# Two accumulator banks from the other pool, a later close, and a fourth weight buffer in a two-layer encoder trunk

## The chip, the cores and the metric

The kernel runs on one core of a Trainium2 chip. The metric is the device time of one execution in microseconds (us), as the median of several runs; smaller is better. The engines are named as in the profile: PE is TensorE (its matmuls), PEld its weight loads, DVE is VectorE, ACT is ScalarE, POOL is GpSimd, and SP is SyncE, which here issues the DMAs.

## The reference

The reference computes two layers of an encoder on 272 tokens (16 learned ones and 256 of the input), 2048 wide, in float32:

```python
def _layer(h, w_in, ..., w_out, ln1_w, ln1_b, w_ff1, w_ff2, ln2_w, ln2_b):
    proj = jnp.einsum('bld,dp->blp', h, w_in)
    ...
    gq, gk, gv, gr, glr, nq, nk, nv = jnp.split(proj, points, axis=-1)
    y_gla = _gla_mixer(gq, gk, gv, gr, glr, gla_w_up, gla_b_up, gla_norm_w)
    y_na = _na_mixer(nq, nk, nv, na_rel_bias).astype(h.dtype)
    mix = jnp.einsum('blm,md->bld', jnp.concatenate([y_gla, y_na], axis=-1), w_out)
    h = _layer_norm(DEEPNORM_ALPHA * h + mix, ln1_w, ln1_b)
    ff = jnp.einsum('blf,fd->bld', jnp.square(jax.nn.relu(jnp.einsum('bld,df->blf', h, w_ff1))), w_ff2)
    return _layer_norm(DEEPNORM_ALPHA * h + ff, ln2_w, ln2_b)
```

`_gla_mixer` is a gated linear attention in both directions with 4 heads (keys 128 wide, values 256 wide). Its output is divided by the root of its mean square over the 256 values of a head and multiplied by a gate. `_na_mixer` is a neighbourhood attention with 16 heads of 64 on a grid of 4 rows by 64 columns; the 16 learned tokens are further keys, and attend among themselves. The learned tokens are dropped from the output, so that the second layer computes most things for 256 tokens only.

## The kernel before

**Weights.** Each weight matrix comes as tiles of 128 by 1024 float32, 512 KB (eight blocks of 128 by 128). `made` (L187) asks for a tile on SP's queue (`raw`), and `halves` (L215) splits it: ACT rounds it to `wh` (L218), DVE computes the rest `wl = raw - wh` (L219). Activations are split in the same way, and a product is made of three matmuls: high by high, high by low, low by high. `raw`, `wh` and `wl` have three buffers each. `weights` (L181) keeps two tiles made: when the matmuls of a tile are written into the program, the next tile's DMA and its two splitting instructions stand ahead of them, and no later tile's.

**Loops.** `by_m` (L317) makes 128 output columns at a time: eight input blocks per tile, one PSUM bank of the pool `pm`, then an eviction. `by_k` (L279) makes 512 output columns at once in four banks and runs over the input blocks two at a time. It stands where the inputs become ready one after the other: the first group of a layer, the first group of the output projection (`w_out`, in the first layer at L304, in the second through `dense`, L314), and one group of the MLP. PSUM has eight banks: four in the pool `pm` (named mm in the profile) and four in the pool `pb` (named bg), which `bank` (L77) hands out.

**Work in between.** Attention is written as generators in two queues. `gla_head` stands in `bg`, and `na_pair`, `silu` and the norms stand in `fg`. `pump` (L127) is called after each weight tile and runs a few steps of both. A step that yields True says that the next one begins with matmuls that wait for results just asked for; the pump then tries to let a weight tile pass between. A bg step's DVE instructions are kept behind the latest `wl` (`issue_after`, L119).

**The end of the attention.** `layer` runs six groups of `by_m` over the projections of the neighbourhood attention. Ahead of the last of these (g == 5) it runs all steps that are left in `bg`, closes the memory of the linear attention (`gctx.close`, L408), and opens that of the norms (`ln_open`, L409), in which `acc` lies. Then comes `by_k(self.y, n, self.mixed)` (L413): `mixed` (L417) runs one step of `fg` ahead of each pair of input blocks, and writes `acc` (L424). While `alone` is true, `spare` (L80) takes the banks of the attention scores from `pm`, else from `pb`. The pump after the last tile of the sixth group runs the output of pair 5 (`na_out`, L851) and the scores of pair 7 (L778), so that the scores' two banks are the latest of `pm` when `by_k` begins. The score banks are read by DVE at L787 and L789; the bank of the last projection tile is read by ACT at L540 and by DVE at L541.

**One head's norm.** In `gla_head` the two halves of a head are squared by ACT into `grs` and `gtn` (L721), multiplied by the gate on DVE (L723), and the squares are added by DVE (L725). `mean` (L976) splits the sum (`sp`: ACT L339, DVE L340) and multiplies it by a matrix of 1/256 on PE (L983).

**The neighbourhood attention's softmax.** `softmax` (L752) takes the maximum on DVE (L754), the exponentials on ACT (L756), the reciprocal on DVE (L757), and multiplies (L760): on POOL for the grid tokens (tiles `ns` and `npr`), on DVE for the learned tokens (tile `nms`, 16 by 96, first layer only). PE transposes `nms` at L808 together with the values (L805, L806).

Of the kernel before, what the change touches and what calls it, by code (L numbers as in the profile page):

```python
# [14 lines left out]
P = 128  # L15
D = 2048
# [42 lines left out]
class Trunk:  # L59
    def __init__(self, ctx, tc, ins, out):  # L60
        self.ctx, self.tc, self.nc = ctx, tc, tc.nc
        self.i, self.out = ins, out
        self.bg, self.fg, self.credit, self.fcredit = deque(), deque(), 0, 0
        self.wants, self.due, self.late, self.low = {}, deque(), 0, True
        self.x = [None] * DC
        self.stream, self.ready = self.order(), deque()
        pool = lambda name, **k: ctx.enter_context(tc.tile_pool(name=name, **k))
        self.cp = pool("const", bufs=1)
        self.xp = pool("xhl", bufs=1)
        self.yp = pool("yhl", bufs=1)  # L70
        self.wp = pool("wst", bufs=3)
        self.jp = pool("jn", bufs=1)
        self.pm = pool("pm", bufs=4, space=PSUM)
        self.pb = pool("pb", bufs=4, space=PSUM)
        self.hp = pool("hop", bufs=2, space=bass.MemoryType.DRAM)
# [8 lines left out]
    def consts(self):  # L84
        nc, c = self.nc, self.cp
        t = lambda n, s, d=F32: c.tile(s, d, name=n, tag=n)
        t("pad", [P, PAD])
        self.vec = t("vec", [P, DEPTH, 66])
        nc.sync.dma_start(self.vec, self.i["vec"].rearrange("l p v -> p l v"))
        self.ident = t("ident", [P, P])  # L90
        nc.sync.dma_start(self.ident, self.i["ident"])
        self.sel = t("sel", [LRK, 2])
        nc.sync.dma_start(self.sel, self.i["sel"])
        self.qmask = t("qmask", [NM, NK2])
        nc.sync.dma_start(self.qmask, self.i["qmask"])
        self.mask = t("mask", [P, 5, 32], U8)
        raw = self.xr.tile([P, 2, L], F32, name="xraw", tag="xraw", bufs=3)[:, 0, :5 * 32].rearrange("p (l c) -> p l c", l=5)
        nc.sync.dma_start(raw, self.i["mask"])
        nc.gpsimd.tensor_copy(self.mask, raw)
        self.ones = {}  # L100
        for n in (GDV, 4 * P, D):
            self.ones[n] = t(f"ones{n}", [P, P])
            nc.gpsimd.memset(self.ones[n], 1.0 / n)
        self.ones_r = {}
        for n in self.ones:
            self.ones_r[n] = t(f"onesr{n}", [P, P], F32R)
            nc.scalar.copy(self.ones_r[n], self.ones[n])
        self.eps = t("eps", [P, 1])
        nc.gpsimd.memset(self.eps, EPS)
        self.one = t("one", [P, 1])  # L110
        nc.gpsimd.memset(self.one, 1.0)
# [68 lines left out]

    def weights(self):  # L181

        while len(self.ready) < 2:
            self.ready.append(self.made(*next(self.stream, (None, (), None))))
        return self.ready.popleft()

    def made(self, ap, ends, kind):  # L187
        if ap is None:
            return None
        nc = self.nc  # L190
        raw = self.wp.tile([P, WB], F32, name="raw", tag="raw")
        wh, wl = (self.wp.tile([P, WIDE], F32R, name=nm, tag=nm) for nm in ("wh", "wl"))
        wh, wl = self.blocks(wh, *HIGHS[kind]), self.blocks(wl, *LOWS[kind])
        for c in map(slice, (0,) + ends, ends):
            self.asked = nc.sync.dma_start(raw[:, c], ap[:, c]).ins
            self.halves(raw[:, c], wh, wl, slice(c.start // P, c.stop // P))
        if not ends:
            self.head(ap, raw, wh, wl)
        return wh, wl
# [76 lines left out]
        self.nc.vector.tensor_tensor(t, t, parts[0], ALU.add)  # L276
        return t

    def by_k(self, acts, n, before, wide=False):  # L279

        ps = [self.pm.tile([P, 512], F32, name="mm", tag="mm") for _ in range(4)]
        if wide:
            ps += [self.bank() for _ in range(4)]
        nk = len(acts)
        for k in range(0, nk, 2):
            before(k)
            if n == T:
                self.dense(ps, acts[k:k + 2], self.weights(), k)
                continue
            for g in range(0, len(ps), 4):  # L290
                wh, wl = self.weights()
                parts = ((wh, 0), (wh, 1), (wl, 0))
                order = [(j, p, m) for j in range(2) for p in range(3) for m in range(4)]
                first = wide and not k
                if first and not g:
                    order.sort(key=lambda o: (o[0], o[2] // 2))
                elif wide and k == 2 and not g:
                    order.sort(key=lambda o: o[1])
                elif first:
                    order.sort(key=lambda o: o[1] // 2)  # L300
                else:
                    order.sort(key=lambda o: (k and o[2], o[1] // 2, o[2]))
                for j, p, m in order:
                    self.nc.tensor.matmul(ps[g + m][:, :n], lhsT=self.block(parts[p][0], 4 * j + m if first else 2 * m + j), rhs=acts[k + j][parts[p][1]][:, :n],  # L304
                                          start=k + j + p == 0, stop=k == nk - 2 and j + p == 3)
        return [[p[:, :T], p[:, T:]] if n == T else [p[:, :n]] for p in ps]
# [46 lines left out]
    def layer(self, l):  # L353
# [4 lines left out]
        with ExitStack() as actx:  # L358
# [20 lines left out]
            with ExitStack() as ectx:  # L379
                self.ep = pool("early", "right", ectx)  # L380
                self.fcredit = 0
                self.fg.append(self.gates())
                if l == 0:
                    with ExitStack() as xctx:
                        self.xr = pool("xr", "right", xctx)
                        first = self.by_k(self.x, L, self.load_x, wide=True)
                    for m in range(4):
                        self.ev_k(m, first.pop(0)[0])
                for m, ps in enumerate(first):
                    self.ev_v(m, ps[0])  # L390
                self.credit, self.alone = 0, True
                self.by_m(self.x, [L] * 4, lambda m, ps: self.ev_v(4 + m, ps), pump=(1, 1, True))
                self.by_m(self.x, [n] * 4, self.ev_q, pump=(1, 1, True))
                self.drain()
            self.a2 = pool("na", "left", bufs=2)
            with ExitStack() as gctx:
# [5 lines left out]
                    self.by_m(self.x, [n] * 4, lambda m, ps: self.ev_r(4 * g + m, ps), pump=(1, GLA_R))  # L402
                self.na_tiles()
                for g in range(6):
                    if g == 5:
                        while self.bg:
                            self.step(self.bg, 1)
                        gctx.close()  # L408
                        self.ln_open()  # L409
                    ns = [n if (4 * g + m) % 3 == 0 else L for m in range(4)]  # L410
                    self.by_m(self.x, ns, lambda m, ps: self.ev_na(4 * g + m, ps), pump=(1, GLA_NA, True))
            self.alone = False
            ps = self.by_k(self.y, n, self.mixed)  # L413
            self.drain()
        self.tail(ps)

# [163 lines left out]
    def gla_head(self, h):  # L580
# [141 lines left out]
            os_.append(g2.tile([P, L], F32, name="on", tag="on")[:, :n])  # L722
            nc.vector.tensor_tensor(os_[e], o, self.gate[2 * h + e], ALU.mult)  # L723
        yield
        nc.vector.tensor_tensor(rs, rs, tn, ALU.add)  # L725
        ms = yield from self.mean(rs, GDV, pool=g2)
        self.newton(rs, ms, self.eps, tn)
        yield
# [8 lines left out]
    def na_tiles(self):  # L737

        def t(name, *shape):
# [4 lines left out]
        self.fetch = lambda: None  # L744
        self.nv = [(self.a2.tile([P, 2, P], F32, name=f"nv{i}", tag=f"nv{i}", bufs=1), t(f"nr{i}", P, 2, 64))
                   for i in range(2)]
        self.npr = [t(f"npr{i}", P, 4, 64) for i in range(2)]
        if self.full:
            self.npm = [t(f"npm{i}", P, 2, NM) for i in range(2)]
            self.nms = [t(f"nms{i}", P, 2, 64) for i in range(2)]  # L750

    def softmax(self, s, st, u, outs, by):  # L752
        nc = self.nc
# [8 lines left out]
    def na_pair(self, c, q, k, v):  # L762
# [3 lines left out]
        bias = b.tile([P, 4, 192], F32, name="nb", tag="nb").rearrange("p u c -> p (u c)")[:, :4 * NKEY]  # L766
        bias = bias.rearrange("p (u c) -> p u c", u=4)
        nc.sync.dma_start(bias, self.i["nab"][self.l, c])
        s = b.tile([P, 4, NKEY], F32, name="ns", tag="ns")
        st = b.tile([P, 12], F32, name="nst", tag="nst")  # L770
        if len(self.due) > 1:
            self.due.popleft()()
# [7 lines left out]
        if self.full:  # L780
            for hh, hs in enumerate(heads):
                nc.tensor.matmul(ps[hh][:NAD, 2 * NKEY:2 * NKEY + NK2], lhsT=q[hs, :NAD], rhs=k[hs, 0, P:],
                                 start=True, stop=True)
            meta = self.nms[c % 2]
            sm = meta[:NM, :, :NK2]
        for hh in range(2):
            nc.vector.tensor_tensor(s[:, 2 * hh:2 * hh + 2, :], two(ps[hh][:, :2 * NKEY]), bias[:, 2 * hh:2 * hh + 2, :], ALU.add)  # L787
            if self.full:
                nc.vector.tensor_tensor(sm[:, hh, :], ps[hh][:NM, 2 * NKEY:2 * NKEY + NK2], self.qmask, ALU.add)  # L789
        pr = self.npr[c % 2]  # L790
        self.softmax(s, st, 4, ((s[:, :, :P], s[:, :, :P]), (pr[:, :, :NK2], s[:, :, P:])), nc.gpsimd)
        yield
        if self.full:
            mt = b.tile([NM, 6], F32, name="mst", tag="mst")
            self.softmax(sm, mt, 2, ((sm, sm),), nc.vector)
        yield
        turned = b.tile([P, 4, 192], F32, name="nt", tag="nb")
        out = lambda at, n: turned[:, :, at:at + 32 * n].rearrange("p j (u c) -> p u j c", c=32)
# [177 lines left out]
    def mean(self, src, n, i=0, pool=None):  # L976
# [3 lines left out]
        yield True  # L980
        p = self.bank()[:, :src.shape[-1]]
        for i, v in enumerate(parts):
            self.nc.tensor.matmul(p, lhsT=self.ones_r[n], rhs=v, start=i == 0, stop=i == 1)  # L983
        return p

    def means(self):
# [140 lines left out]
    def ln_out(self):  # L1127
# [2 lines left out]


        nc, lp, acc = self.nc, self.lp, self.acc
        ident, one = self.ident, self.ones[D]
        t = lambda nm, s, d=F32: lp.tile(s, d, name=nm, tag=nm)
        blocks = [(g, h) for g in range(4) for h in range(2)]
        bank = [self.pm.tile([P, 512], F32, name="mm", tag="mm") for _ in range(4)]
# [145 lines left out]
```

## Time and profile before

| | |
|---|---|
| median of 3 runs | 2322.85 us (2322.03 to 2323.60) |
| profiled execution, its own time | 2323.91 us |
| its span | 2322.1 us |
| PE busy | 2304.2 us (99%), 18420 matmuls |
| DVE busy | 1526.4 us (66%) |
| ACT busy | 1223.0 us (53%) |
| POOL busy | 155.4 us (7%) |
| DMA | 431.65 MB, mean 186 GB/s |

Times are counted from the start of the span. The second layer begins at about 1190 us. The attention and what goes with it lies at about 53 to 364 us and at about 1246 to 1540 us; the rest is projections and the MLP. A busy PE is not a PE at its peak, since the ends of matmuls are modelled; a wait of PE shows as idle time ahead of a matmul, with the instruction that ended it.

### The profile page before, as it was taken

To read this page: it belongs to the slowest core of one execution; us is meant where nothing else is said; L and a number is where in the kernel's file an instruction comes from. 1 tells how busy PE (TensorE), PEld (TensorE's weight loads), DVE (VectorE), ACT (ScalarE), POOL (GpSimd) and SP (SyncE) were. 2 spreads that over 40 slices of the span, in tenths; PEclk is the share of its full clock that TensorE was granted. 3 is DMA by queue.
4 is the path that set the end of the run, shared out by engine and by line. 5 is a ranking of instruction groups with operands and counts; after the bars stand their busy time and mean duration, and the time that the engine had idled before them with its cause. 6 is when DMAs were issued, how large, how long until landed. Compare 5 with 4: busy or idle time off the path is not lost.

```text
span 2322.1 us, 45272 instructions
## 1 busy us (share of the span) xinstructions
PE 2304.2 (99%) x18420; PEld 2188.9 (94%) x18420; DVE 1526.4 (66%) x2408; ACT 1223.0 (53%) x2096; POOL 155.4 (7%) x232
## 2 busy tenths in 40 slices
PE   9999999999999999999999999999999999999998
PEld 9999999999999999999999899889988888888888
DVE  5588878875544455547576788688866555666655
ACT  5666655564433344444456766655654334555443
POOL 0023210100000000000020122200100000000000
PEclk9999999999999999999999999999999999999999
DMA  8556666565555556665655556665666666667664
GB/s 259 155 164 184 199 189 177 173 181 181 182 181 178 179 181 182 180 179 178 182 173 173 173 175 209 195 187 181 198 191 196 194 191 193 192 196 218 195 195 150
DMA packets 129824, 431.65 MB, mean 186 GB/s; under 512 B 14792, under 2 KB 23496, under 8 KB 129616
## 3 DMA queue, kind: packets, MB, share of 16 engines
q1 hardware_dynamic: 127024, 421.95, 59.9%
q10 hardware_dynamic: 2592, 6.82, 0.8%
q8 instruction: 144, 2.36, 0.4%
q14 instruction: 64, 0.52, 0.1%
HBM read 420.32 MB, written 8.39 MB: 185 GB/s over the span
## 4 chain that ended last, share of the span: by engine, by line
PE 91%; DVE 5%; ACT 2%; issue 1%; DMA 1%; POOL 0%; DVEq 0%; ACTq 0%; SPq 0%
PE mm L253 53%; PE mm L265 29%; PE mm L304 4%; PE mm L314 2%; DVE wl L219 1%; PE bg L304 1%; ACT wh L218 1%; ACT ns L756 0%; DVE S L615 0%; PE bg L851 0%; PE bg L470 0%; PE bg L629 0%; DVE acc L1085 0%; POOL dec L617 0%; DMA raw<-in_wff 0%
## 5 line engine op out<-in xcount | busy, mean ns | idle before, releaser
L219 DVE TENSOR_TENSOR wl<-raw,wh 128x1024 fp32r<-128x1024 f32 (+1 forms) x770 | 935.9, 1223 | 621.8 <-ACT wh L218 518.5
L218 ACT CAST wh<-raw 128x1024 fp32r<-128x1024 f32 (+1 forms) x770 | 804.7, 1047 | 755.8 <-PE mm L253 352.6
L253 PE MATMUL mm<-x,wh 128*128 128x272 f32 (+3 forms) x4544 | 806.8, 294 | 0.0
L253 PEld LDWEIGHTS mm<-x,wh 128*128 128x128 f32 x4544 | 648.0, 188 | 15.5 <-issue 0.8
L253 PE MATMUL mm<-x,wl 128*128 128x272 f32 (+3 forms) x2432 | 520.6, 285 | 2.9 <-DVE wl L219 2.9
L253 PEld LDWEIGHTS mm<-x,wl 128*128 128x128 f32 x2432 | 391.4, 188 | 3.4 <-DVE wl L219 3.4
L253 PE MATMUL mm<-y,wh 128*128 128x272 f32 (+1 forms) x1440 | 235.0, 285 | 0.0
L253 PEld LDWEIGHTS mm<-y,wh 128*128 128x128 f32 x1440 | 199.7, 188 | 0.1
L265 PE MATMUL mm<-x,wh 128*128 128x512 f32 x832 | 193.8, 390 | 0.0
L265 PEld LDWEIGHTS mm<-x,wh 128*128 128x128 f32 x832 | 154.3, 188 | 31.0
L253 PE MATMUL mm<-u,wh 128*128 128x272 f32 (+1 forms) x1056 | 172.1, 285 | 0.0
L265 PE MATMUL mm<-y,wh 128*128 128x512 f32 x688 | 162.3, 389 | 0.0
L265 PEld LDWEIGHTS mm<-y,wh 128*128 128x128 f32 x688 | 128.7, 188 | 26.8 <-issue 0.4
L253 PE MATMUL mm<-y,wl 128*128 128x272 f32 (+1 forms) x720 | 146.5, 284 | 0.0
L253 PEld LDWEIGHTS mm<-u,wh 128*128 128x128 f32 x1056 | 146.3, 188 | 0.0
L265 PE MATMUL mm<-u,wh 128*128 128x512 f32 x496 | 118.3, 391 | 0.0
L253 PEld LDWEIGHTS mm<-y,wl 128*128 128x128 f32 x720 | 112.5, 188 | 0.0
L265 PEld LDWEIGHTS mm<-u,wh 128*128 128x128 f32 x496 | 90.9, 188 | 17.6
L253 PE MATMUL mm<-u,wl 128*128 128x272 f32 (+1 forms) x528 | 107.4, 284 | 0.0
L265 PEld LDWEIGHTS mm<-x,wl 128*128 128x128 f32 x832 | 98.5, 188 | 2.1
L265 PE MATMUL mm<-x,wl 128*128 128x256 f32 x832 | 99.0, 276 | 0.0
L265 PEld LDWEIGHTS mm<-y,wl 128*128 128x128 f32 x688 | 84.3, 188 | 2.8
(275 smaller groups left out, 2285.0 us busy)
## 6 DMA issues: line engine op xcount, KB each, us to landing
raw<-in_wff SPq DMA_DIRECT2D x512, 512.0 KB, 3.6
raw<-in_win SPq DMA_DIRECT2D x190, 512.0 KB, 4.2
raw<-in_wout SPq DMA_DIRECT2D x64, 512.0 KB, 3.9
hop<-nt ACTq DMA_DIRECT2D x16, 384.0 KB, 2.3
np<-hop SPq DMA_DIRECT2D x64, 96.0 KB, 4.1
nb<-in_nab SPq DMA_DIRECT2D x16, 352.0 KB, 4.4
xraw<-in_xT SPq DMA_DIRECT2D x7, 272.0 KB, 5.8
out<-out SPq DMA_DIRECT2D x5, 256.0 KB, 3.1
```

The source lines that it names most:

```text
L218: self.nc.scalar.copy(h, r)
L219: self.wl = self.nc.vector.tensor_tensor(lo, r, h.bitcast(F32), ALU.subtract).ins
L253: mm(o, lhsT=self.block(w, j), rhs=rhs, start=first and not i, stop=last and i == len(TURNS[once]) - 1)
L265: self.nc.tensor.matmul(o, lhsT=self.block(both[j // 8][low], j % 8), rhs=rhs, start=first and not i + j, stop=bool(last and i and j == 15 ...
L304: self.nc.tensor.matmul(ps[g + m][:, :n], lhsT=self.block(parts[p][0], 4 * j + m if first else 2 * m + j), rhs=acts[k + j][parts[p][1]][:, ...
L314: self.nc.tensor.matmul(o, lhsT=self.block(both[low], i), rhs=rhs, start=not low and k + i % 2 == 0, stop=k == DC - 2 and i % 2 == 1 and n ...
```

## The change

- **Weight buffers.** `wh` and `wl` get four buffers; `raw` keeps three. `weights` keeps `self.lead` tiles made: two until the first k-outer group of the first layer is written, three after it.
- **Two banks of the other pool.** In the first group of the output projection, `by_k` takes its first two banks from `pb` and the other two from `pm`. In the first layer its first pair of input blocks is ordered by bank, as the later pairs were already.
- **A later close.** The rest of `bg` is run, and the memory closed and opened, in the middle of the sixth group (after two of its four output tiles), no longer ahead of it.
- **Two operations moved to POOL.** The sum of the squares of a head (L725, 8 times), and the last multiplication of the learned tokens' softmax (L760 on `nms`, 8 times, first layer).
- **Memory.** The matrices of 1/n are kept once, in float32r, and read as float32 where that is wanted. `ns`, `npr` and `nms` have one buffer instead of two.

```diff
-        self.stream, self.ready = self.order(), deque()
+        self.stream, self.ready, self.lead = self.order(), deque(), 2
...
-            self.ones[n] = t(f"ones{n}", [P, P])
-            nc.gpsimd.memset(self.ones[n], 1.0 / n)
-        self.ones_r = {}
-        for n in self.ones:
-            self.ones_r[n] = t(f"onesr{n}", [P, P], F32R)
-            nc.scalar.copy(self.ones_r[n], self.ones[n])
+            one = self.ones[n] = t(f"ones{n}", [P, P], F32R)
+            nc.gpsimd.memset(one.bitcast(F32), 1.0 / n)
+            nc.scalar.copy(one, one.bitcast(F32))
...
-        while len(self.ready) < 2:
+        while len(self.ready) < self.lead:
...
-        wh, wl = (self.wp.tile([P, WIDE], F32R, name=nm, tag=nm) for nm in ("wh", "wl"))
+        wh, wl = (self.wp.tile([P, WIDE], F32R, name=nm, tag=nm, bufs=4) for nm in ("wh", "wl"))
...
-    def by_k(self, acts, n, before, wide=False):
-
-        ps = [self.pm.tile([P, 512], F32, name="mm", tag="mm") for _ in range(4)]
+    def by_k(self, acts, n, before, wide=False, ends=False):
+
+        tile = lambda n: [self.pm.tile([P, 512], F32, name="mm", tag="mm") for _ in range(n)]
+        ps = [self.bank(), self.bank()] + tile(2) if ends else tile(4)
...
-                    order.sort(key=lambda o: (k and o[2], o[1] // 2, o[2]))
+                    order.sort(key=lambda o: ((k or ends) and o[2], o[1] // 2, o[2]))
...
                         first = self.by_k(self.x, L, self.load_x, wide=True)
+                        self.lead = 3
...
-                    if g == 5:
-                        while self.bg:
-                            self.step(self.bg, 1)
-                        gctx.close()
-                        self.ln_open()
                     ns = [n if (4 * g + m) % 3 == 0 else L for m in range(4)]
-                    self.by_m(self.x, ns, lambda m, ps: self.ev_na(4 * g + m, ps), pump=(1, GLA_NA, True))
+                    for at in ((0, 2), (2, 4)) if g == 5 else ((0, 4),):
+                        if at == (2, 4):
+                            while self.bg:
+                                self.step(self.bg, 1)
+                            gctx.close()
+                            self.ln_open()
+                        self.by_m(self.x, ns[slice(*at)], lambda m, ps: self.ev_na(4 * g + at[0] + m, ps), pump=(1, GLA_NA, True))
             self.alone = False
-            ps = self.by_k(self.y, n, self.mixed)
+            ps = self.by_k(self.y, n, self.mixed, ends=True)
...
-        nc.vector.tensor_tensor(rs, rs, tn, ALU.add)
+        nc.gpsimd.tensor_tensor(rs, rs, tn, ALU.add)
...
-            self.softmax(sm, mt, 2, ((sm, sm),), nc.vector)
+            self.softmax(sm, mt, 2, ((sm, sm),), nc.gpsimd)
...
-            self.nc.tensor.matmul(p, lhsT=self.ones_r[n], rhs=v, start=i == 0, stop=i == 1)
+            self.nc.tensor.matmul(p, lhsT=self.ones[n], rhs=v, start=i == 0, stop=i == 1)
```

More of the change, by code (lines that the diff above doesn't have):

```diff
@@ L746, in na_tiles @@
                    for i in range(2)]
-        self.npr = [t(f"npr{i}", P, 4, 64) for i in range(2)]
+        self.npr = t("npr", P, 4, 64)
         if self.full:
             self.npm = [t(f"npm{i}", P, 2, NM) for i in range(2)]
-            self.nms = [t(f"nms{i}", P, 2, 64) for i in range(2)]
+            self.nms = t("nms", P, 2, 64)
     def softmax(self, s, st, u, outs, by):
@@ L768, in na_pair @@
         nc.sync.dma_start(bias, self.i["nab"][self.l, c])
-        s = b.tile([P, 4, NKEY], F32, name="ns", tag="ns")
+        s = b.tile([P, 4, NKEY], F32, name="ns", tag="ns", bufs=1)
         st = b.tile([P, 12], F32, name="nst", tag="nst")
@@ L783, in na_pair @@
                                  start=True, stop=True)
-            meta = self.nms[c % 2]
+            meta = self.nms
             sm = meta[:NM, :, :NK2]
@@ L789, in na_pair @@
                 nc.vector.tensor_tensor(sm[:, hh, :], ps[hh][:NM, 2 * NKEY:2 * NKEY + NK2], self.qmask, ALU.add)
-        pr = self.npr[c % 2]
+        pr = self.npr
         self.softmax(s, st, 4, ((s[:, :, :P], s[:, :, :P]), (pr[:, :, :NK2], s[:, :, P:])), nc.gpsimd)
@@ L1132, in ln_out @@
         nc, lp, acc = self.nc, self.lp, self.acc
-        ident, one = self.ident, self.ones[D]
+        ident, one = self.ident, self.ones[D].bitcast(F32)
         t = lambda nm, s, d=F32: lp.tile(s, d, name=nm, tag=nm)
```

## The prediction

> **What bounds the kernel now.** I read the page first: who is busy, and for what share of the span.
>
> ```profile
> span 2322.1 us, 45272 instructions
> PE 2304.2 (99%) x18420; PEld 2188.9 (94%) x18420; DVE 1526.4 (66%) x2408; ACT 1223.0 (53%) x2096; POOL 155.4 (7%) x232
> ```
>
> PE is idle for 2322.1 - 2304.2 = 17.9 us in all. The change leaves out no matmul, so it can only bring idle time of PE and what follows from it. The second view is therefore the list of waits, for PE alone (us in total, times, longest):
>
> ```profile
> PE bg L983 <- ACT sp L339: 3.3, 3, 1.2
> PE mm L253 <- DVE wl L219: 2.9, 2, 2.3
> PE bg L444 <- DVE zero L441: 1.2, 1, 1.2
> PE mm L314 <- DVE nr L541: 0.9, 1, 0.9
> PE mm L304 <- DVE nr L541: 0.8, 1, 0.8
> PE mm L304 <- DVE nms L789: 0.8, 1, 0.8
> PE bg L808 <- DVE nms L760: 0.7, 1, 0.7
> PE mm L304 <- DVE fx L1122: 0.7, 1, 0.7
> ```
>
> Most lines have a part of the change opposite: L983 the sum of squares on POOL and the later close; `wl` the fourth buffer; `nr` and L789 the banks; L808 the softmax's product on POOL. These come to 3.3 + 2.9 + 0.9 + 0.8 + 0.8 + 0.7 = 9.4 us. `zero` is the start, and `fx` belongs to another k-outer group: the change touches neither. The third view is a table of stretches, which says where the waits lie (start and end, length, then busy time of PE, PEld, DVE, ACT and POOL, and the granted clock):
>
> ```profile
> 200.00:340.00 140.00, 136.50 (x1651) 133.46 (x1651) 112.83 (x265) 91.28 (x239) 35.87 (x54) 1.00 0.65 199
> ...
> 1365.00:1515.00 150.00, 145.72 (x1604) 135.93 (x1603) 113.93 (x213) 98.73 (x244) 33.13 (x58) 0.99 0.64 197
> ```
>
> The two attention stretches lose 3.5 and 4.3 us with DVE busy for 81% and 76% of them. There a queue of small work on DVE makes PE wait now and then. The long stretch between loses next to nothing, so a deeper weight buffer has nothing to win in it:
>
> ```profile
> 507.00:1190.00 683.00, 682.98 (x5587) 682.76 (x5586) 366.77 (x452) 292.88 (x393) 2.21 (x9) 1.00 0.60 181
> ```
>
> **The fourth weight buffer.** The longest wait and the `wl` that ended it, from the timeline, then the other wait of this kind, from the timeline of PE:
>
> ```profile
> 1456.10 1.23 DVE L219 TENSOR_TENSOR wl<-raw,wh 128x1024 fp32r<-128x1024 f32 x1
> ...
> 1457.39 0.52 PE L253 MATMUL mm<-x,wl 128*128 128x272 f32 x2 [2.32 <-DVE wl L219]
> ```
>
> ```profile
> 278.46 0.52 PE L253 MATMUL mm<-x,wl 128*128 128x272 f32 x2 [0.62 <-DVE wl L219]
> ```
>
> Two equal stretches behind the first of them, and from the chain of waits one weight tile on PE:
>
> ```profile
> 1459.10:1461.90 2.80, 2.80 (x14) 2.80 (x14) 2.24 (x3) 1.11 (x3) 0.00 (x0) 0.50 0.66 192
> 1462.30:1465.10 2.80, 2.80 (x25) 2.80 (x24) 1.25 (x2) 0.76 (x2) 1.14 (x2) 1.00 0.86 297
> ```
>
> ```profile
> 29.23 2.93 PE mm L304 x24
> ```
>
> Just after the wait the granted clock is 0.50, and PE starts 14 matmuls in the time in which it then starts 25: another 2.80 x (1 - 14/25) = 1.2 us at least. A tile is 2.93 us of PE. With four buffers a split may run as early as before (when PE is done with the same earlier tile), but PE needs its result one tile later. Lateness of 2.32 and 0.62 us, below 2.93, is covered: 2.32 + 0.62 + 1.2 = 4.1 us. The bounds are 0, if it is the raw tile that comes late, since `raw` keeps three buffers, and 4.1. I take 4.1, because both rows name DVE's `wl`, and the `wl` at 1456.10 came from a busy DVE. The Trainium skill, "TensorE: Matmul & The Clock Gate", under "Why this matters for your kernels", asks for no idle gaps above about 3 us; by that a gap of 2.32 us leaves the clock alone, and this part is 2.9 us. The row with 0.50 behind such a gap speaks against it.
>
> With the tile its DMA request moves ahead on SP's queue, past about one tile's worth of bias loads and `np` fetches. It waits for the split of the tile three back, as before, so the queue stands no longer. Steps of the heads on DVE that are kept behind the latest `wl` are now behind a later tile's, which runs at the moment at which the former one did. Both cost nothing as long as raw tiles land in time.
>
> **The sum of squares on POOL, and the later close.** What stood ahead of the three waits at L983 (timeline: a `wl`, the second square, the sum):
>
> ```profile
> 301.11 2.36 DVE L219 TENSOR_TENSOR wl<-raw,wh 128x1024 fp32r<-128x1024 f32 x2
> ...
> 302.48 0.41 ACT L721 ACTIVATE gtn<-bg 128x272 f32<-128x272 f32 x1
> ...
> 304.66 0.43 DVE L725 TENSOR_TENSOR grs<-grs,gtn 128x272 f32<-128x272 f32 x1
> ```
>
> ```profile
> 1326.98 1.23 DVE L219 TENSOR_TENSOR wl<-raw,wh 128x1024 fp32r<-128x1024 f32 x1 [0.93 <-ACT wh L218]
> 1327.12 0.37 ACT L721 ACTIVATE gtn<-bg 128x256 f32<-128x256 f32 x1
> ...
> 1328.79 0.41 DVE L725 TENSOR_TENSOR grs<-grs,gtn 128x256 f32<-128x256 f32 x1
> ```
>
> ```profile
> 1482.17 1.23 DVE L219 TENSOR_TENSOR wl<-raw,wh 128x1024 fp32r<-128x1024 f32 x1 [0.29 <-ACT wh L218]
> ...
> 1482.58 0.38 ACT L721 ACTIVATE gtn<-bg 128x256 f32<-128x256 f32 x1
> ...
> 1484.18 0.41 DVE L725 TENSOR_TENSOR grs<-grs,gtn 128x256 f32<-128x256 f32 x1
> ```
>
> The addends are there at 302.89, 1327.49 and 1482.96; the sum is made at 305.09, 1329.20 and 1484.59, because DVE has other work in between. What such a sum takes on POOL, and what POOL and DVE do to each other:
>
> ```profile
> 342.19 1.04 POOL L760 TENSOR_TENSOR ns<-ns,nst 128x512 f32<-128x512 f32 x1 [6.74 <-DVE nst L757]
> ...
> 342.56 0.78 DVE L760 TENSOR_TENSOR nms<-nms,mst 16x96 f32<-16x96 f32 x1
> ...
> 343.18 0.52 POOL L760 TENSOR_TENSOR npr<-ns,nst 128x192 f32<-128x192 f32 x1
> ```
>
> ```profile
> L760 DVE TENSOR_TENSOR nms<-nms,mst x8: 203/204/775, 200.9 to 342.6; 16x96 f32<-16x96 f32 x8
> ```
>
> ```profile
> 212.74 2.86 POOL L617 TENSOR_TENSOR dec<-dec 128x136 f32<-128x136 f32 x1 [4.85 <-DVE S L615]
> ```
>
> Between 0.52 us for 192 columns and 1.04 for 512, I estimate 0.65 us for 272 (DVE: 0.43). But beside POOL the small DVE product took 0.78 instead of 0.20 and ended just after POOL's, and one POOL product of 136 columns took 2.86. So I let POOL begin when the running `wl` ends, at 303.47, 1328.21 and 1483.40. The sums are made at 304.12, 1328.86 and 1484.05: earlier by 0.97, 0.34 and 0.54, together 1.9 us. The later close lets weight tiles pass between the last head's steps (the waits at 305 and 1485 are the last heads'); I add 0.4. The bounds are 3.3 (all of it) and a loss of 1.2 us for each of the three, by a second `wl`. The other five sums wait for nothing now; I charge 0.3 for all. Net 2.3 - 0.3 = 2.0. In POOL's queue the sum can also stand behind a pair's `ns` and `npr` (1.04 + 0.52 us); that is within the loss just named. The close comes four weight tiles later, and `acc` opens later by as much, but its first write belongs to `by_k`, behind the sixth group: nothing, unless the last head is late.
>
> **The banks, and the softmax's product on POOL.** In the first layer 0.8 + 0.8 us of waits for `pm` banks go: the first two banks are free in `pb`, and by the time the third is due (12 matmuls, 1.5 us) those of `pm` are. But the wait behind them is for the product at L760, whose inputs do not come sooner by themselves. PE reaches L808 1.6 us earlier and waits 1.6 us more. On POOL the product also stands behind `npr`, which ends at 343.70, where on DVE it ended at 343.34. Against that, the exponentials' ACT queue was held by PE, so the inputs may come sooner:
>
> ```profile
> 338.94 1.05 ACT L218 CAST wh<-raw 128x1024 fp32r<-128x1024 f32 x1 [2.34 <-PE mm L304]
> ```
>
> The bounds are a gain of 2.3 (waits 0.8 + 0.8 + 0.7) and a loss of 0.7; I take 0. In the second layer there is no such product, and the 0.9 us at L314 goes: 0.9, with bounds 0 and 0.9. `by_k` now keeps two of four `pb` banks until its end. The value transposes and the outputs of pairs 6 and 7 share the other two, from evictions with this distance:
>
> ```profile
> 344.43 0.35 DVE L817 COPY npm<-bg 64x16 f32<-64x16 f32 x2
> ```
>
> ```profile
> 346.43 0.89 PE L851 MATMUL bg<-np,v 64*64 64x128 f32 x24
> ```
>
> The last eviction ends 1.65 us ahead of the next use: nothing, or a few tenths if PE is early. The single buffers for `ns`, `npr` and `nms` cost nothing, since one pair's readers end before the next pair's scores are made. The matrices of 1/n are made by as many instructions as before.
>
> **The sum:** 4.1 + 2.0 + 0 + 0.9 = 7.0 us. The profiled execution took 2323.91 us (1.8 above its span), so 2316.9; it stood 1.06 above the median of 2322.85, so the median becomes 2315.9. By the clock rule above it would be 2317.1. With all bounds at their best the gain is 4.1 + 3.3 + 2.3 + 0.9 = 10.6: 2312.2.
>
> **The rivals.**
>
> *POOL in the chain makes it slower.* Each sum may meet two `wl` as the product at 212.74 did. At 2.86 us behind its addends it is made at 305.75, 1330.35 and 1485.82, which is 0.66 + 1.15 + 1.23 = 3.0 us later than now; and the other five heads lose up to 2.86 - 0.43 = 2.4 us each, 12 us, where ACT stands at `sp` with the next `wh` behind it. Then 15.0 - 4.1 - 0.9 = 10 us slower: 2332.9. It decides from about 1.3 us for each of the five. The row of 0.78 speaks for it, the 2.93 us tile that mostly lies between the sum and L983 against it. The Trainium skill, "SBUF — State Buffer", under "SBUF: two separate sides", says that GpSimd and a VectorE operation with two SBUF inputs exclude each other for a whole instruction; the rows of 0.78 and 2.86 agree.
>
> *The waits move.* DVE at 81% and 76% is the true limit in the attention, and PE, freed, waits at the next step, as I expect at L808. Then only the clock and the bank of the second layer are left: 1.2 + 0.9 - 0.3 = 1.8, 2321.0. For it: chains of small steps feed PE. Against it: DVE does have a fifth of the time free.
>
> *The lead does nothing.* Three raw buffers bound how far splits run ahead. Then 4.1 is lost: a gain of 2.9, 2320.0. For it is this line of the waits, against it that none of PE's rows names a raw tile:
>
> ```profile
> ACT wh L218 <- DMA raw<-in_win: 22.5, 18, 2.6
> ```
>
> **How the numbers follow.** Forecast 60%, slower through POOL 13%, waits move 17%, lead does nothing 10%. A difference of 0.2% (4.6 us) is about what a measurement of this kernel can tell from none. The forecast counts as faster; the two middle rivals, at 1.8 and 2.9 us, as the same; POOL's as slower. The forecast's own range is 2312.2 to 2318.2, from all bounds at their best to where it begins to count as the same. The range of 2311.5 to 2322.0 takes in the two middle rivals and leaves out POOL's.
>
> **What would show it.** In the changed profile PE's waits on `wl` are gone from the attention, with the clock at 1.00 around 1455 us; L304 and L314 do not wait for `nr` or L789; L983 waits below 1.5 us in all; L808 waits about 2 us, on POOL. It is wrong if waits on `wl` are as long as before (the lead), if L983 waits above 4 us and POOL's L725 takes above 1.5 us (the lock), or if new lines of several tenths stand in PE's list (moved).

## The result, and the profile after

The changed kernel takes 2316.57 us (median of 7 runs, 2315.38 to 2318.05), the kernel before 2323.32 us beside it (median of 7, 2322.03 to 2324.58). The ratio is 0.9971 (95% interval 0.9962 to 0.9980): 6.75 us faster, where 7.0 us were forecast. The profiled execution took 2316.10 us, 7.8 us less than the profiled one of before: this one lies 0.5 us below its median, that one 0.6 us above. What can move single executions by a microsecond or two is told at the end. Lines move by up to 3 in the changed kernel: L253 is now L250, L219 is L216, L304 is L302, L314 is L312, L339 is L337.

The head of its page, and the list of PE's waits (us in total, times, longest):

```profile
span 2314.3 us, 45228 instructions
...
PE 2300.4 (99%) x18420; PEld 2186.8 (94%) x18420; DVE 1519.4 (66%) x2392; ACT 1224.6 (53%) x2096; POOL 160.4 (7%) x245
```

```profile
PE bg L808 <- POOL nms L760: 2.9, 3, 2.3
PE bg L444 <- DVE zero L441: 1.2, 1, 1.2
PE mm L312 <- DVE nr L541: 0.9, 1, 0.9
PE mm L302 <- DVE fx L1122: 0.7, 1, 0.7
PE bg L851 <- DVE v L812: 0.6, 1, 0.6
PE bg L983 <- ACT sp L337: 0.5, 1, 0.5
PE bg L716 <- ACT parts L337: 0.5, 1, 0.5
PE bg L717 <- DVE parts L338: 0.3, 1, 0.3
```

PE's idle time fell from 17.9 to 13.9 us. Against the list of before: the waits on `wl` are gone (2.9 before), L983 waits 0.5 instead of 3.3, and L304's two waits for `pm` banks are gone. L808 waits 2.9 instead of 0.7. L312 waits for `nr` as long as L314 did (0.6 us in a second profile of the same kernel, below). L851, L716 and L717 are new, 1.4 us together. The same matmuls also keep PE busy for 3.8 us less; at least 1.2 us of that is the half clock near 1457 us, which is not there any more (third column from the right), and where the rest comes from, no view here says:

```profile
1450.00:1460.00 10.00, 10.00 (x84) 10.00 (x83) 8.28 (x15) 6.75 (x13) 2.69 (x6) 1.00 0.47 148
```

How the gain grows can be read from the same matmuls in both timelines of PE, first before, then after:

```profile
333.78 0.77 PE L304 MATMUL mm<-y,wh 128*128 128x272 f32 x4
...
343.48 0.30 PE L808 MATMUL bg<-ident,nms 128*128 128x128 f32 x1 [0.70 <-DVE nms L760]
...
1514.10 0.50 PE L314 MATMUL mm<-y,wh 128*128 128x512 f32 x1 [0.89 <-DVE nr L541]
```

```profile
331.76 0.77 PE L302 MATMUL bg<-y,wh 128*128 128x272 f32 x4
...
340.92 0.33 PE L808 MATMUL bg<-ident,nms 128*128 128x128 f32 x1 [2.29 <-POOL nms L760]
...
1507.59 0.73 PE L312 MATMUL mm<-y,wh 128*128 128x512 f32 x2 [0.90 <-DVE nr L541]
```

At the first output projection PE is 2.02 us ahead, at the transposes behind its first two pairs 2.56, and at the second output projection 6.51. So the first layer gives 2.6 us, the second layer's attention some 4, and what is left of the 7.8 us builds up behind it.

### The profile page after: what moved, and what is told of

Read it like the earlier page. It is cut to its first block, busy times and chain, and to the rows that moved or that the text cites. A ratio compares the mean times of both kernels' runs of the same rounds, so it can differ in the third digit from the quotient of the medians.

```text
span 2314.3 us, 45228 instructions
## 1 busy us (share of the span) xinstructions
PE 2300.4 (99%) x18420; PEld 2186.8 (94%) x18420; DVE 1519.4 (66%) x2392; ACT 1224.6 (53%) x2096; POOL 160.4 (7%) x245
## 4 chain that ended last, share of the span: by engine, by line
PE 79%; DVE 3%; ACT 1%; issue 1%; DMA 0%; POOL 0%; DVEq 0%; ACTq 0%; POOLq 0%; SPq 0%
PE mm L250 44%; PE mm L262 30%; PE mm L302 2%; PE mm L312 1%; DVE wl L216 1%; PE bg L312 0%; ACT wh L215 0%; PE bg L302 0%; DMA raw<-in_win 0%; DVE acc L1085 0%; PE bg L851 0%; DVE S L615 0%; ACT ns L756 0%; PE bg L983 0%; PE bg L470 0%
## 5 line engine op out<-in xcount | busy, mean ns | idle before, releaser
L216 DVE TENSOR_TENSOR wl<-raw,wh 128x1024 fp32r<-128x1024 f32 (+1 forms) x770 | 936.3, 1223 | 619.8 <-ACT wh L215 518.4
L250 PE MATMUL mm<-x,wh 128*128 128x272 f32 (+3 forms) x4544 | 805.3, 294 | 0.0
L250 PEld LDWEIGHTS mm<-x,wh 128*128 128x128 f32 x4544 | 646.8, 188 | 15.4 <-DVE gtn L577 0.3
L250 PE MATMUL mm<-x,wl 128*128 128x272 f32 (+3 forms) x2432 | 519.6, 284 | 0.0
L250 PEld LDWEIGHTS mm<-x,wl 128*128 128x128 f32 x2432 | 390.8, 188 | 0.0
L250 PE MATMUL mm<-y,wh 128*128 128x272 f32 (+1 forms) x1440 | 235.0, 285 | 0.0
L250 PEld LDWEIGHTS mm<-y,wh 128*128 128x128 f32 x1440 | 199.7, 188 | 0.1
L250 PE MATMUL mm<-u,wh 128*128 128x272 f32 (+1 forms) x1056 | 172.1, 285 | 0.0
L250 PE MATMUL mm<-y,wl 128*128 128x272 f32 (+1 forms) x720 | 146.4, 284 | 0.0
L250 PEld LDWEIGHTS mm<-u,wh 128*128 128x128 f32 x1056 | 146.3, 188 | 0.0
L250 PEld LDWEIGHTS mm<-y,wl 128*128 128x128 f32 x720 | 112.5, 188 | 0.0
L262 PEld LDWEIGHTS mm<-u,wh 128*128 128x128 f32 x496 | 90.9, 188 | 17.7
L250 PE MATMUL mm<-u,wl 128*128 128x272 f32 (+1 forms) x528 | 107.3, 284 | 0.0
```

What stands on the lines that cost most here:

```text
L216: self.wl = self.nc.vector.tensor_tensor(lo, r, h.bitcast(F32), ALU.subtract).ins
L250: mm(o, lhsT=self.block(w, j), rhs=rhs, start=first and not i, stop=last and i == len(TURNS[once]) - 1)
L262: self.nc.tensor.matmul(o, lhsT=self.block(both[j // 8][low], j % 8), rhs=rhs, start=first and not i + j, stop=bool(last and i and j == 15 ...
```

## The experiments

All were timed against the kernel before on the same chip. The forecast rested on waits that can be added up one by one. The rival is that waits only move, because PE, freed at one place, arrives early at the next.

**The lead alone.** The kernel before, with the buffers and the lead, and the smaller memory that makes room for them:

```diff
+        self.stream, self.ready, self.lead = self.order(), deque(), 2
...
+        while len(self.ready) < self.lead:
...
+        wh, wl = (self.wp.tile([P, WIDE], F32R, name=nm, tag=nm, bufs=4) for nm in ("wh", "wl"))
...
+                        self.lead = 3
```

> The kernel before with the fourth buffers and the lead of three alone (and the smaller memory they need). If the two waits on wl and the half clock behind one of them are what the lead takes away, and nothing takes their place: 0.8 us at 278 and 4.2 us at 1457, so 5 us off, about 2318.3 us, no wait of PE on wl and a clock of 1.00 around 1457 us, with the waits at L983, L304, L314 as in the kernel before. If the waits only move to the next step: less than 2 us off.

Measured: 2321.83 us (11 runs), ratio 0.9997 (0.9989 to 1.0006): not told from no change (the medians lie 1.1 us apart). PE's waits in its profile:

```profile
PE bg L981 <- ACT sp L336: 4.2, 3, 2.2
PE bg L806 <- DVE nms L758: 1.3, 2, 0.7
PE bg L442 <- DVE zero L439: 1.2, 1, 1.2
PE bg L714 <- ACT parts L336: 1.1, 1, 1.1
PE mm L311 <- DVE nr L539: 0.9, 1, 0.9
PE mm L301 <- DVE nr L539: 0.8, 1, 0.8
PE mm L301 <- DVE nms L787: 0.8, 1, 0.8
```

The waits on `wl` are gone, as forecast. But two steps of the last head, behind the place where `wl` was late, took most of it back (timeline of PE):

```profile
1475.67 0.38 PE L714 MATMUL bg<-parts,V 128*128 128x256 f32 x1 [1.14 <-ACT parts L336]
```

```profile
1483.35 0.38 PE L981 MATMUL bg<-sp,ones 128*128 128x256 f32 x1 [2.18 <-ACT sp L336]
```

In the kernel before, the first of these did not wait, and the second waited 0.97 us (at L983, 1485.08). PE came early and stood for the head's norm instead. Its idle time is 17.7 us, against 17.9 before. Taken alone, the lead is the rival's case. (This kernel also has the single buffers of `ns`, `npr` and `nms`; what they cost was not timed apart.)

**Everything but the lead**, then **the buffers without the lead**:

```diff
-                        self.lead = 3
```

(The first of the two also goes back to three buffers.)

> The changed kernel with three buffers and a lead of two, everything else as changed. If the parts add up: 2316.6 + 5 = about 2321.5 us, and the wait on wl near 1455 us is back, with a clock of 0.50 behind it. If the sums on POOL relieve DVE enough by themselves: no wait on wl above 1 us, and about 2317.5 us.

> The changed kernel with four buffers, but a lead of two throughout. If it is the place of the splits in ACT's and DVE's queues that counts (a tile earlier), the fourth buffer alone brings little: within 1.5 us of the kernel without the lead, about 2321 us. If PE's late release of a buffer was what held the splits, the buffer alone is enough: about 2316.6 us.

Measured without both: 2320.88 us (11 runs), ratio 0.9988 (0.9979 to 0.9996). The wait and the half clock behind it are back, so the sums on POOL do not spare DVE enough:

```profile
PE mm L250 <- DVE wl L216: 2.4, 1, 2.4
```

```profile
1457.20:1460.20 3.00, 3.00 (x15) 3.00 (x14) 2.90 (x4) 1.22 (x3) 0.05 (x1) 0.50 0.71 201
```

The same step is thus worth 0.03% when it is alone, and 0.17% on top of the others (0.9988 against 0.9971, some 4 us), or 0.14% (some 3 us) by the second measurement of the changed kernel below (0.9974). Each ratio is known to about 0.09% either way, so that the times alone hardly separate the two worths; the waits do. With the buffers but a lead of two: 2318.59 us (11 runs), ratio 0.9977 (0.9968 to 0.9986). The time lies between the two that I had named and is not told from the changed kernel's. The place in the queues is not what counts: L250 waits for `wl` nowhere. PE's release of the buffer was what held the split. What the lead adds shows only in the k-outer groups, from 53 us on:

```profile
PE mm L302 <- DVE wl L216: 0.5, 1, 0.5
...
PE mm L302 <- ACT wh L215: 0.3, 1, 0.3
```

**The lead from the first tile on.**

```diff
-        self.stream, self.ready, self.lead = self.order(), deque(), 2
+        self.stream, self.ready, self.lead = self.order(), deque(), 3
```

> The changed kernel with a lead of three from the first tile on. If the first group is fed by DMA and by splits that come just in time, a third tile ahead stands in the queues of SP, ACT and DVE before the activations' pieces: 1 to 3 us slower than the changed kernel, 2317.6 to 2319.6 us, lost before 53 us. If the first group has room: 2316.6 us.

Measured: 2318.52 us (11 runs, 2316.66 to 2321.16), ratio 0.9978 (0.9969 to 0.9986). The changed kernel's interval overlaps it. A loss of up to 2 us is possible, but this does not show it. Its one profile points that way: PE waits 0.9 us for an input that ACT splits (`x`, at 12.41 us), and the first tile behind the first group (L250) begins at 53.73 us, where the other 12 profiles have 51.95 to 53.25.

**The sum of squares back on DVE; the early close back.**

```diff
-        nc.gpsimd.tensor_tensor(rs, rs, tn, ALU.add)
+        nc.vector.tensor_tensor(rs, rs, tn, ALU.add)
```

```diff
-                    for at in ((0, 2), (2, 4)) if g == 5 else ((0, 4),):
-                        if at == (2, 4):
+                    for at in ((0, 4),):
+                        if g == 5:
```

> The changed kernel with the sum of squares back on DVE. The changed kernel waits 0.5 us at L983, the one with the lead alone 4.2 us. If it is POOL that took these waits away: 2 to 3 us slower than the changed kernel (2316.6), about 2319, with waits at L983 near 3 us, above all in the last head of the second layer and at 1326 us. If it is the later close: below 1 us slower, and the wait at the last heads stays away.

> The changed kernel with the close ahead of the sixth group, as in the kernel before. If the later close is what keeps the last heads' norm from being run in one go: waits at L983 of 1 to 2 us come back at the last head of each layer, 2318 to 2319 us. If the sum on POOL is enough: 2316.6 us and no wait at L983 above 0.6 us.

Measured: 2317.61 us with the sum on DVE (8 runs), ratio 0.9974 (0.9964 to 0.9984), and 2317.84 us with the early close (10 runs), ratio 0.9977 (0.9968 to 0.9986). The times hardly tell them apart; the waits at L983 do, first with the sum on DVE, then with the early close:

```profile
PE bg L983 <- ACT sp L337: 0.8, 1, 0.8
```

```profile
PE bg L983 <- ACT sp L337: 2.1, 2, 1.6
```

Beside POOL's sum the close takes away 1.6 us, and beside the close POOL's sum takes away 0.3. But each does part of the other's work: with neither, in the kernel with the lead alone, these waits come to 4.2 us (L981), so that POOL's sum by itself removes about 2 and the close by itself about 3. (That kernel differs from these two in the banks and the softmax's product as well.) On POOL the sum is in fact slower than on DVE (0.41 to 0.43 us in the run with the sum on DVE), as the answer for its line in the changed kernel shows (minimum, median, maximum in ns):

```profile
L725 POOL TENSOR_TENSOR grs<-grs,gtn x8: 738/774/1227, 145.0 to 1478.5; 128x272 f32<-128x272 f32 x4, 128x256 f32<-128x256 f32 x4
```

Three of the eight (at 302.51, 1324.81 and 1478.46 us) begin 0.3 to 0.6 us ahead of the end of a `wl` on DVE, and take 1.16, 1.23 and 0.94 us. Each of them ends 0.6 us after that `wl`. The slowest, from the timeline:

```profile
1324.21 1.23 DVE L216 TENSOR_TENSOR wl<-raw,wh 128x1024 fp32r<-128x1024 f32 x1 [0.93 <-ACT wh L215]
...
1324.81 1.23 POOL L725 TENSOR_TENSOR grs<-grs,gtn 128x256 f32<-128x256 f32 x1 [1.14 <-ACT gtn L721]
```

**The softmax's product back on DVE.**

```diff
-            self.softmax(sm, mt, 2, ((sm, sm),), nc.gpsimd)
+            self.softmax(sm, mt, 2, ((sm, sm),), nc.vector)
```

> The changed kernel with the product of the learned tokens' softmax back on DVE. If its place in POOL's queue behind npr is what it costs: the wait at L808 is 0.6 us shorter at 341 us and gone at 217 and 299 us, together 1.3 us off, about 2315.3 us. If its inputs come too late in any case: no change of the wait of 2.3 us, 2316.6 us.

Measured: 2315.00 us (5 runs, 2314.56 to 2316.08), ratio 0.9966 (0.9952 to 0.9979). The long wait at L808 is shorter by 0.6 us, as expected. Of the two short ones, which I expected to go, only that at 217 us went; the one at 299 us grew from 0.2 to 0.6 us, so that L808 waits 2.3 us in all, 0.6 less and not 1.3:

```profile
PE bg L808 <- ACT wh L215: 1.7, 1, 1.7
...
PE bg L808 <- DVE nms L760: 0.6, 1, 0.6
```

(The `wh` that it names has nothing to do with the product; it is only what ended last before. The product ended at 340.35 us, 0.15 ahead of L808; in the kernel before these were 0.14 apart.) I put the rest of the wait down to the early arrival of PE. The median is 1.6 us below the changed kernel's; the intervals overlap.

**Four banks from `pm` again.**

```diff
-            ps = self.by_k(self.y, n, self.mixed, ends=True)
+            ps = self.by_k(self.y, n, self.mixed)
```

> The changed kernel with all four banks of the output projection's first group from pm, in the former order. If the 1.6 us that the banks save in the first layer is only waited for at L808 instead: the waits at L304 (0.8 and 0.8) come back, L808's falls by as much, and nothing changes: 2316.6 us, or a few tenths less without the wait of 0.6 us at L851. If the banks bring what the waits said: 1.6 us or more slower.

Measured: 2317.93 us (10 runs), ratio 0.9977 (0.9968 to 0.9986), not told from the changed kernel.

```profile
PE bg L808 <- POOL nms L760: 1.6, 2, 1.2
PE mm L312 <- DVE nr L541: 1.2, 1, 1.2
...
PE mm L302 <- DVE nms L789: 0.8, 1, 0.8
PE mm L302 <- DVE nr L541: 0.8, 1, 0.8
```

The two waits of 0.8 are back, and L808's longest falls from 2.3 to 1.2. In the first layer the banks' gain is handed on to L808 for the most part. In the second, L312 waits 1.2 us, more than in either profile of the changed kernel.

**PE later at L808, on top of the product on DVE.**

```diff
     def mixed(self, k):
-        self.pump(1, 0)
+        if k or not self.full:
+            self.pump(1, 0)
```

> The changed kernel with the softmax's product on DVE, and in the first layer no step of the attention ahead of the first pair of the output projection, so that the transposes at L808 come one weight tile (2.9 us) later. If L808's wait of 1.7 to 2.3 us is only a matter of PE coming too early: it is gone, no half clock near 341 us in any run, 1.7 us off the kernel with the product on DVE (2315.0), about 2313.3 us. If it is handed on to the outputs of pair 7 at the end of the group (the last pair of blocks waits for them): a new wait of 1 us or more near 357 us, and 2315 us.

Measured: 2313.76 us (5 runs, 2313.45 to 2314.03), ratio 0.9960 (0.9947 to 0.9972), the fastest of all. The changed kernel, run again beside it:

> The changed kernel once more, beside the two others on the same chip: 2316.6 us. If the gap of 2.3 us at L808 sometimes halves the clock for 3.4 us behind it and sometimes not, as the profiles with and without it show, its runs spread by about 1.5 us more than those of the two kernels without that gap.

2317.50 us (8 runs, 2315.18 to 2319.02), ratio 0.9974 (0.9963 to 0.9984). No run of either lies in the range of the other. With the step one tile later, L808's long wait is gone (the line is L809 here), and only 0.5 us at 299 us is left. The step was not timed without the product on DVE, and the interval overlaps that of the product alone (0.9952 to 0.9979); what each is worth is read from the waits, 1.7 and 0.6 us:

```profile
PE mm L312 <- DVE nr L542: 0.7, 1, 0.7
PE bg L852 <- DVE v L813: 0.6, 1, 0.6
PE bg L984 <- ACT sp L337: 0.5, 1, 0.5
PE bg L809 <- DVE nms L761: 0.5, 1, 0.5
```

**The second layer's fourth bank last, on top of that.**

```diff
+        order = [(low, i) for low in ((0, 1) if k % 4 == 0 else (1, 0)) for i in range(8)]
+        if k == 0:
+            order.sort(key=lambda o: o[1] // 2 == 3)
+        for low, i in order:
...
```

> The same, and in the second layer the fourth bank's matmuls of the first pair come behind the low parts of the other three (6 matmuls of 0.11 us later). If the wait on nr at L312 is there because the fourth bank is due only 6 matmuls after the start: 0.3 to 0.7 us of it go, and 0.5 us off. If the eviction at L541 is later by itself: the wait stays.

Measured: 2315.84 us (6 runs, 2314.21 to 2319.77), ratio 0.9972 (0.9960 to 0.9983): no better. Three runs lie at 2314.2 to 2314.5, just above the kernel without this step, and three at 2317.2 to 2319.8. The wait on `nr` is gone from the list, but PE, earlier by as much, stands at the outputs of pair 6, which want the bank that the values of pair 7 still hold:

```profile
PE bg L854 <- DVE v L815: 1.3, 1, 1.3
...
PE bg L854 <- DMA np<-hop: 0.7, 1, 0.7
```

## Why the prediction was right, step by step

The mechanism held: waits of PE that could be named beforehand are gone. The closeness of 7.0 and 6.75 us is in part luck. Of the 7.0, 1.2 were the clock and 5.8 were waits. Measured in the two profiles, PE's idle time fell by 4.0 us and its busy time by 3.8, of which a step at half clock explains some 1.5 (see the last section). The other 2 us or so have no account here.

- **The buffer, 4.1 us: about right in size, wrong in what it hangs on.** Both waits and the half clock went, and on top of the other parts it is worth some 3 to 4 us. But alone it was worth 0.03%, since L981 and L714 took it back. The rival *the waits move* describes the part alone. With either the later close or the sum on POOL in place, most of the gain stays (0.9974 and 0.9977). *The lead does nothing* fails for buffer and lead together; for a lead of three on top of four buffers no gain is shown.
- **The sum and the close, 2.0 us: right sum, wrong as two separate terms.** The step that failed is adding 1.9 us for three sums made earlier on POOL and 0.4 for the close as if they had nothing to do with each other. The waits at L983 fell from 3.3 to 0.5 us. With the sum on DVE they are 0.8, with the early close 2.1: beside the close, POOL's sum is worth 0.3 us, and the close 1.6 beside POOL's sum. The price of the sum on POOL was right: I had 0.65 us from the end of the running `wl`, and it was 0.6.
- **The banks and the product in the first layer, 0 us: right.** The waits of 0.8 and 0.8 went, and L808's longest grew from 0.7 to 2.3 ("about 2"). The loss that I set at up to 0.7 for the product on POOL is there: 0.6 us of that wait.
- **The 0.9 us at L314: wrong.** In the two profiles of the changed kernel 0.9 and 0.6 us of it stand. I had taken it that the bank becomes free when it did before. The bank is wanted 1.65 us after the group's start, where it was wanted after 0.73, so 0.9 us later, as meant. But its reader on DVE (L541) also comes 0.9 us later: 3.7 us behind the last projection matmul, where it was 2.7, since it stands behind a `wl` of 1.23 us that itself begins later. PE and DVE in the changed kernel:

```profile
1503.28 0.41 PE L250 MATMUL mm<-x,wl 128*128 128x272 f32 x2
...
1505.04 1.20 PE L312 MATMUL bg<-y,wh 128*128 128x512 f32 x4
1506.07 0.62 PE L312 MATMUL mm<-y,wh 128*128 128x512 f32 x2
```

```profile
1506.21 1.23 DVE L216 TENSOR_TENSOR wl<-raw,wh 128x1024 fp32r<-128x1024 f32 x1 [1.21 <-ACT wh L215]
1507.35 0.18 DVE L541 COPY nr<-mm 128x32 f32<-128x32 f32 x1
```

In the kernel before, the last projection matmuls end at 1511.14, the group begins at 1512.48, and L541 stands at 1513.87.

- **The bank supply, "a few tenths": 0.6 us** at L851. The new waits at L716 and L717 (0.8) were not forecast. They offset what the part on L983 brought beyond its 2.0.
- **POOL slower:** no. Its sums take up to 1.23 us, not 2.86, and a weight tile mostly lies between them and L983. That DVE's `wl` can hold POOL up shows in the three sums that run into one. Behind the slowest of these lies the 0.5 us that PE still waits at L983 (1326.53 us).

## What to carry to other kernels

A list of one engine's waits shows where a change can gain, but the terms do not simply add: for each wait that goes, ask what that engine reaches next and when its inputs are made. A deeper buffer that does next to nothing alone can be worth most of its price once the next wait behind it is taken away. Two changes that shorten the same wait must not be priced as if each stood alone. When an engine begins to wait at a moved step, moving that step one tile back is worth a try: here it took away 1.7 us of waiting, where faster inputs took 0.6.

## What the hardware showed that was not expected

The clock near L808 differs between runs of the same kernel with the same wait. From the tables of stretches, the changed kernel's second profile, with a wait of 2.23 us, and its first, with one of 2.29 us:

```profile
341.70:344.70 3.00, 3.00 (x16) 3.00 (x15) 2.05 (x6) 0.37 (x3) 0.00 (x0) 0.50 0.71 231
```

```profile
345.50:348.50 3.00, 3.00 (x27) 3.00 (x26) 2.16 (x6) 1.59 (x5) 0.00 (x0) 1.00 0.44 122
```

The second row shows the full rate on such matmuls, 27 in 3 us, a little behind L808 in the first profile; the clock is 1.00 there throughout. In the second profile 16 begin in 3 us. The same matmuls, from L808 to the next L851, show what this costs: 2.88 us in the first profile, 4.42 in the second, so 1.5 us more.

```profile
340.92 0.33 PE L808 MATMUL bg<-ident,nms 128*128 128x128 f32 x1 [2.29 <-POOL nms L760]
...
343.80 0.89 PE L851 MATMUL bg<-np,v 64*64 64x128 f32 x24
```

```profile
341.14 0.33 PE L808 MATMUL bg<-ident,nms 128*128 128x128 f32 x1 [2.23 <-POOL nms L760]
...
345.56 0.89 PE L851 MATMUL bg<-np,v 64*64 64x128 f32 x24
```

The two executions took 2316.10 and 2317.61 us. In all 13 profiles the changes of the clock lie on a grid of 3.413 us, whose place differs from run to run. I added up, from the records of PE's matmuls, its idle time in each step of the grid. It is 2.10, 2.10, 2.22, 2.23, 2.35 and 2.37 us in the six steps that are followed by a step at half clock (apart from the end of the kernel), and at most 1.84 us in all others. So, in these profiles, a wait of 2.2 to 2.4 us is followed by 3.4 us at half clock if 2.1 us or more of it fall into one step. The 2.29 us at L808 in the first profile straddle two, with 1.67 and 0.62 us, and no half clock follows. The Trainium skill, "TensorE: Matmul & The Clock Gate", under "What's actually happening", has that free-running window; the traces agree on its length, but here 2.1 us of idle time in it were enough.

How much of the spread of the times this explains is open. I had expected the changed kernel's runs to spread by 1.5 us more than those of the two kernels without the long wait at L808. On the same chip, they spread over 3.8 us in eight runs, and those of the kernel with the step one tile later over 0.6 us in five, which fits. But the kernel with the fourth bank last spread over 5.6 us in six, which does not, and one step at half clock costs only 1.5 us. The mean clock that was recorded for each run points to the clock in part: 1.000 in the four shorter and 0.999 in the three longer of the changed kernel's first seven runs, and 0.998 in the two longest with the fourth bank last. In the changed kernel's second set it does not tell the runs apart (0.999 in the two shortest as in the longest). The start varies as well, by the 1.3 us named above for the first tile behind the first group.
